# Down and output projection of a two-superblock trunk in the 4+4-sum seven-product form, with sums kept in PSUM, weight sums by DRAM transfers and activation sums made beside the up-projection

## The chip, the cores and the metric

The kernel runs on one core of a Trainium2 chip. The metric is the device time of one execution in microseconds; three runs of the kernel before gave a median of 2719.7 us (2719.38 to 2721.61). Engines are named as in the profile: PE does matmuls (PEld loads their weights), DVE, ACT and POOL work elementwise, SP only issues transfers. ACT and POOL issue transfers too, and all of these queues run in order.

## What is computed

One layer of a mixer block and a gated feed-forward network on a 2048 x 1024 input, in float32:

```python
xn = rmsnorm(x, norm1_g)
z = xn @ w_in                              # pool channels, q, f, i, o, gates
ya = pool_mixer(u_pool, ...) @ w_pa
yb = hgrn2_mixer(zq, zf, zi, zo, ...) @ w_pb
merged = gates[0] * ya + gates[1] * yb
x = x + merged @ w_o                       # output projection, 1024 x 1024
h = rmsnorm(x, norm2_g) @ w_up             # 1024 x 5632, then a causal conv of width 3
x = x + (silu(gate) * val) @ w_down        # down projection, 2816 x 1024
out = rmsnorm(x, final_g)
```

## The kernel before

**Stages.** The sequence is worked in two superblocks of 1024 rows, each of two blocks (`hf` 0 and 1) of 512 rows. For each superblock the stages are: `io` (two of the input projections, `proj_io`), `in` (14 units of the other input projections, with the recurrence and the pooling as tasks beside them), `pa` and `pb` (branch projections and gating), `wo` (output projection), `up` (22 units of the up-projection, with conv and gate in `emit_up`) and `dn` (down projection, with the final norm). All large products are done as seven half-size products (Strassen's or Winograd's form) of two-part float32r operands: an operand is cast to a high part on ACT and the low part is subtracted on DVE (`split`, L561 and L562, for activations; `Stream.convert`, L207 and L208, for weights), and each product of tiles takes three matmuls (`n_step`, `chain_t`).

**Weights.** `Stream` holds the planned order of all weight tiles. `load` (L185) issues a 128 x 512 tile (256 KB) into one of 8 `raw` buffers on the SP queue, `convert` makes `ops` from it, at most 4 tiles ahead of PE's use and in 6 buffers. For `wo` and `dn`, `plan_n_step` makes the sums of two weight quarters on POOL (L430), five per row step k. For `up` and the second superblock's `io` and `in`, the sums of weight quarters come from DRAM: the class `Sums` makes them with eight dependent transfers for each group of four units, four plain copies on ACT's queue (L263) and four adding transfers on POOL's queue (L260), each of about 1 MB. `Sums.make` starts a task for a whole weight matrix; the task runs one transfer every `SUM_LAG` = 4 ticks (a tick is six large matmuls), going over all groups before the next dependent step. The `up` sums (6 groups, tiles su0 to su5) start when the first `io` stage ends, the `io` and `in` sums (so, si) when the first `up` stage starts. A weight tile that needs sums that are not made finishes the whole task at once (`join`).

**Output and down projection.** `Rows` runs `wo` (4 row steps k) and `dn` (11 steps). `DOWN` and `W_OUT` list passes of one or two of the seven products M1 to M7. `make` adds or subtracts two activation tiles on POOL (L1010), five per k, and splits the result; `run` multiplies, and after the last k adds each product from PSUM into one to two of the four output quarters on DVE (L1038): 12 additions for each of 4 row tiles. The last `hold` steps of a pass are run row tile by row tile. The gated activations of `up` go to DRAM (`dg`, 44 tiles in each superblock) and are fetched again (`g`, L760).

**Order.** Tasks are stepped by ticks while PE's matmuls are recorded; a scheduler then orders the instructions of each engine by its own estimate of times. At run time each engine and each queue takes its instructions strictly in that order.

Of the kernel before, what the change touches and what calls it, by code (L numbers as in the profile page):

```python
# [33 lines left out]
B12, B22, B21, B11 = 0, 1, 2, 3  # L34
PROD = {
    "M1": ("M1", ((0, 0, 1), (1, 1, 1)), ((B11, 1), (B22, 1)), ((0, 0, 1), (1, 1, 1))),
    "M2": ("M2", ((1, 0, 1), (1, 1, 1)), ((B11, 1),), ((1, 0, 1), (1, 1, -1))),
    "M3": ("M3", ((0, 0, 1),), ((B12, 1), (B22, -1)), ((0, 1, 1), (1, 1, 1))),
    "M4": ("M4", ((1, 1, 1),), ((B21, 1), (B11, -1)), ((0, 0, 1), (1, 0, 1))),
    "M5": ("M5", ((0, 0, 1), (0, 1, 1)), ((B22, 1),), ((0, 0, -1), (0, 1, 1))),  # L40
    "M6": ("M6", ((1, 0, 1), (0, 0, -1)), ((B11, 1), (B12, 1)), ((1, 1, 1),)),
    "M7": ("M7", ((0, 1, 1), (1, 1, -1)), ((B21, 1), (B22, 1)), ((0, 0, 1),)),
}


def passes(*names):
    return [[PROD[n] for n in p.split()] for p in names]


DOWN = passes("M3 M6", "M5 M7", "M4 M1", "M2")  # L50
W_OUT = passes("M3 M5", "M7 M4", "M1", "M2", "M6")

# [14 lines left out]
LEADS = 2, 5, 4  # L67
# [7 lines left out]
SUM_LAG = 4  # L75
# [6 lines left out]
def tile_trunk(  # L82
# [37 lines left out]
    count = [0]  # L120
# [26 lines left out]
    def mm(*args, **kw):  # L147
        pe.matmul(*args, **kw)  # L148
        count[0] += 1
        if count[0] % MM_PER_TICK == 0:  # L150
            tick()
# [79 lines left out]

    stream = Stream()

    class Sums:


        def __init__(self, name, groups):

            self.name, self.groups = name, groups
            self.where = {}  # L240
            self.task = None
# [5 lines left out]
        def make(self):  # L247
            def gen():
                n = len(self.groups)
                for g, (units, _) in enumerate(self.groups):  # L250
                    for k in ("s1", "s2", "s3", "s4"):
                        nm = f"{self.name}{g}{k}"
                        self.t[g, k] = dram.tile([P, len(units), 512], F32, tag=nm, name=nm)
                for dst, src, add in (("s1", 2, 0), ("s3", 2, 0), ("s1", 3, 1), ("s3", 0, 1),
                                      ("s2", "s1", 0), ("s2", 0, 1), ("s4", "s2", 0),
                                      ("s4", 1, 1)):
                    for g in range(n):
                        x = self.t[g, src] if isinstance(src, str) else self.groups[g][1][src]
                        if add:
                            pool.dma_start(self.t[g, dst], x, accum_op=ALU.add)  # L260
                        else:
                            with tc.issue_after(stream.mark.ins):
                                act.dma_start(self.t[g, dst], x)  # L263
                        yield SUM_LAG

            self.task = Task(gen())
# [60 lines left out]
    def plan_mixer(b0):  # L327
# [8 lines left out]
        plan_n("wo", w_o, W_OUT, KD // 2)  # L336
# [63 lines left out]
    def plan_ffn():  # L400
# [6 lines left out]
        plan_n("dn", w_dn, DOWN, MF // 2)  # L407

    def plan_n(key, src, passes, nk):
        for prods in passes:  # L410
            for k in range(nk):
                plan_n_step(key, src[k], prods)

    def plan_n_step(key, rows, prods):
        where = {}
        for q in sorted({q for pr in prods for q, _ in pr[2]}):
            where[q] = stream.raw(rows[:, q * 512 : (q + 1) * 512])

        def view(q):
            return where[q].tile  # L420

        for pr in prods:
            terms = pr[2]

            def fn(nm, terms=terms):
                if len(terms) == 1:
                    return view(terms[0][0])
                t = slot(f"{nm}b")
                op = ALU.add if terms[1][1] > 0 else ALU.subtract
                pool.tensor_tensor(t, view(terms[0][0]), view(terms[1][0]), op)  # L430
                return t

            stream.op(key, fn, [where[q] for q, _ in terms])
# [11 lines left out]

    io_q = w_io.rearrange("k p c -> p k c")
    sums["up"] = Sums("su", [group_up(m0) for m0 in range(0, MF, GROUP)])
    sums["io"] = Sums("so", [(list(range(4)),
# [537 lines left out]
    class Rows:  # L986
        def __init__(self, name, key, passes, nk, get, acc, ahead=0):
            self.name, self.key, self.passes, self.nk = name, key, passes, nk
            self.get, self.acc, self.ahead = get, acc, ahead
            self.steps = [(i, k) for i in range(len(passes)) for k in range(nk)]  # L990
            self.made = 0
            self.a = {}

        def make(self, upto):
            while self.made < min(upto, len(self.steps)):
                i, k = self.steps[self.made]
                for n in range(self.made, min(self.made + self.ahead, len(self.steps))):
# [496 lines left out]
```

## Time and profile before

The profiled execution took 2723.2 us, of which the span (first to last instruction) is 2721.5 us. The table is read from the profile's view of busy time by stretches, cut at the first matmul of each stage.

| stage | superblock 0, us | superblock 1, us |
|---|---|---|
| start and `io` | 117 | 82 |
| `in` | 389 | 353 |
| `pa` and `pb` | 90 | 90 |
| `wo` | 92 | 92 |
| `up` | 468 | 446 |
| `dn` | 251 | 243 |
| after the last matmul | | 8.5 |

A stage is read by comparing it with the time of its own matmuls, and with the busy time of DVE and POOL in the same stretch. The share of the 16 transfer engines' time ("DMA share") and the granted PE clock stand in the same rows.

### The profile page before, as it was taken

The page shows a single profiled execution, that of the slowest core. Times are in us where ns is not written, and L with a number is a line of the kernel's source. Part 1 is how long each engine was busy: PE and PEld are TensorE (multiplying, and loading weights), DVE is VectorE, ACT ScalarE, POOL GpSimd, SP SyncE. Part 2 cuts the span into 40 slices and gives each one's busy share as a digit, 9 for nine tenths or more (in the row PEclk, how much of TensorE's full clock was granted, in tenths as well). Part 3 has the DMA queues.
Part 4 walks back from the last instruction along what each step waited for, and adds up shares of the span by engine and source line. Part 5 has one row for each costly group of instructions (what it writes and reads, how often), then busy time and mean ns, then how long its engine had stood idle before and what let it go on. Part 6 is the DMA issues. An engine that isn't in the chain of part 4 may idle for free.

```text
span 2721.5 us, 35290 instructions
## 1 busy us (share of the span) xinstructions
PE 2571.2 (94%) x11464; PEld 2072.5 (76%) x11464; DVE 2190.7 (80%) x3414; ACT 1166.9 (43%) x2204; POOL 1113.3 (41%) x1171
## 2 busy tenths in 40 slices
PE   7989998999799999989999999999999999998898
PEld 6777777887578888767878788888777888885686
DVE  7879779579687777799987777674898777778998
ACT  5324333423454444443364344342345544444344
POOL 5544344076442111197761111211853211117785
PEclk9999999999899999999999999999999999999999
DMA  6797569654999543474465344347443433436552
GB/s 213 216 265 194 153 192 236 212 192 153 284 262 284 165 127 118 143 262 132 159 198 159 97 124 128 113 150 246 164 146 94 126 121 123 121 123 227 196 168 85
DMA packets 254472, 467.50 MB, mean 172 GB/s; under 512 B 24688, under 2 KB 41200, under 8 KB 253936
## 3 DMA queue, kind: packets, MB, share of 16 engines
q1 hardware_dynamic: 207840, 356.08, 41.1%
q0 software_dynamic: 21184, 41.95, 8.7%
q10 hardware_dynamic: 25264, 67.23, 6.6%
q8 instruction: 90, 1.47, 0.2%
q14 instruction: 94, 0.77, 0.1%
HBM read 391.75 MB, written 157.29 MB: 202 GB/s over the span
## 4 chain that ended last, share of the span: by engine, by line
PE 60%; DVE 16%; DMA 7%; issue 5%; POOL 5%; ACT 2%; SPq 0%; ACTq 0%; DVEq 0%; POOLq 0%
PE up_Z L148 13%; PE up_X L148 8%; PE up_V L148 8%; DVE ops L208 5%; PE gr_Z L148 4%; PE pa L148 3%; PE pb L148 3%; PE gr_X L148 2%; PE gr_V L148 2%; PE dn_M L148 2%; PE fr_Z L148 2%; DMA g<-dg 1%; PE fr_X L148 1%; PE io_Z L148 1%; DMA su3s<-in_w_up_t 1%
## 5 line engine op out<-in xcount | busy, mean ns | idle before, releaser
L207 ACT CAST ops<-raw 128x512 fp32r<-128x512 f32 x582 | 358.5, 620 | 716.2 <-PE up_Z L148 240.0
L208 DVE TENSOR_TENSOR ops<-raw,ops 128x512 fp32r<-128x512 f32 x582 | 450.7, 780 | 124.1 <-ACT ops L207 119.1
L1296 POOL COPY hist<-h 128x2 f32<-128x2 f32 x88 | 38.3, 435 | 403.5 <-DVE h L942 402.9
L1301 DVE SCALAR_TENSOR_TENSOR e<-h,cols,e 128x512 f32<-128x512 f32 x176 | 136.3, 794 | 18.8 <-ACT e L1299 13.8
L1299 ACT ACTIVATE e<-h,cols 128x512 f32<-128x512 f32 x176 | 138.1, 812 | 19.0 <-DVE h L940 11.7
L1303 DVE SCALAR_TENSOR_TENSOR e<-h,cols,e 128x512 f32<-128x512 f32 x176 | 136.0, 777 | 1.3
L1294 POOL COPY h<-h 128x2 f32<-128x2 f32 x88 | 38.0, 458 | 152.1 <-DVE h L940 148.6
L1232 POOL TENSOR_TENSOR ya<-ya,gl 128x512 f32<-128x512 f32 x32 | 47.2, 1486 | 106.8 <-DVE gl L1231 106.8
L979 DVE TENSOR_TENSOR up_u<-up_Z,up_e 128x512 f32<-128x512 f32 x44 | 30.4, 690 | 66.8 <-PE up_Z L148 64.9
L1134 POOL TENSOR_TENSOR q<-q,qs 128x512 f32<-128x512 f32 x16 | 23.3, 1456 | 131.9 <-ACT qs L1133 94.1
L1307 ACT ACTIVATE e<-e 128x512 f32<-128x512 f32 x88 | 55.3, 629 | 40.6 <-DVE e L1303 40.6
L809 POOL COPY qm<-q 128x64 f32<-128x64 f32 x64 | 25.8, 457 | 109.5 <-DVE q L874 21.6
L1171 ACT ACTIVATE gt<-gt,cols 128x512 f32<-128x512 f32 x48 | 34.8, 726 | 74.0 <-DVE gt L942 58.0
L1038 DVE TENSOR_TENSOR ac<-ac,dn_M 128x512 f32<-128x512 f32 x96 | 59.9, 679 | 3.6 <-PE dn_M L148 3.6
L1038 DVE TENSOR_TENSOR x<-x,wo_M 128x512 f32<-128x512 f32 x96 | 61.1, 678 | 0.4
L940 DVE TENSOR_TENSOR h<-up_Z,up_e 128x512 f32<-128x512 f32 x44 | 30.4, 691 | 38.1 <-PE up_Z L148 38.0
L942 DVE TENSOR_TENSOR h<-up_u,up_V 128x512 f32<-128x512 f32 x88 | 60.0, 682 | 0.1
L817 PE MATMUL pl<-qm,k 128*128 128x192 f32 x256 | 48.7, 332 | 8.0 <-DVE f L835 3.1
L817 PEld LDWEIGHTS pl<-qm,k 128*128 128x128 f32 x256 | 43.1, 191 | 13.1 <-issue 4.6
L148 PE MATMUL dn_M<-ops,dn_M_0h 128*128 128x512 f32 x112 | 39.3, 425 | 13.9 <-DVE ops L208 5.5
L1294 POOL COPY h<-hist 128x2 f32<-128x2 f32 x88 | 52.2, 642 | 0.0
L1308 DVE TENSOR_TENSOR e<-e,e 128x512 f32<-128x512 f32 x72 | 51.6, 717 | 0.4
(1743 smaller groups left out, 9025.4 us busy)
## 6 DMA issues: line engine op xcount, KB each, us to landing
raw<-in_w_dn SPq DMA_DIRECT2D x198, 256.0 KB, 3.6
raw<-in_w_up_t SPq DMA_DIRECT2D x132, 256.0 KB, 3.2
raw<-in_w_in_t SPq DMA_DIRECT2D x98, 256.0 KB, 3.6
dg<-e SPq DMA_DIRECT2D x88, 256.0 KB, 3.5
g<-dg SPq DMA_DIRECT2D x88, 256.0 KB, 5.3
raw<-in_w_o SPq DMA_DIRECT2D x80, 256.0 KB, 3.6
raw<-in_w_io SPq DMA_DIRECT2D x68, 256.0 KB, 4.9
x<-in_x SPq DMA_DIRECT2D x64, 256.0 KB, 5.3
```

The lines of the kernel that those rows point to most:

```text
L148: pe.matmul(*args, **kw)
L207: self.mark = act.copy(hi, v)
L208: dve.tensor_tensor(lo, v, f32(hi), ALU.subtract)
L817: pe.matmul(pa_[:, c * 192 : c * 192 + 192], ks[:, (i + c) * P : (i + c + 1) * P], mv[:, c].rearrange("p s x -> p (s x)"), start=True, sto ...
L942: dve.tensor_tensor(dst, t, ps, ALU.add if how == "add" else ALU.subtract)
L1038: dve.tensor_tensor(t, t, ps[pr[0], j], ALU.add if sg > 0 else ALU.subtract)
L1294: pool.tensor_copy(h[:, 0:2], hist[:, mt] if hf == 0 else hs[s, 0][:, TB : TB + 2])
L1299: act.activation(t, h[:, 2:], AF.Identity, bias=col(o_cb + mt), scale=col(o_cw + 4 * MF + mt))
L1301: dve.scalar_tensor_tensor(t, h[:, 1 : 1 + TB], col(o_cw + 2 * MF + mt), t, ALU.mult, ALU.add)
L1303: dve.scalar_tensor_tensor(t, h[:, 0:TB], col(o_cw + mt), t, ALU.mult, ALU.add)
L1307: act.activation(g, g, AF.Silu)
L1308: (pool if m < G_POOL else dve).tensor_tensor(g, g, ts[0, hf], ALU.mult)
```

## The change

`wo` and `dn` use Winograd's form (products P1 to P7, four weight sums and four activation sums), in which partial sums of products stay in PSUM: a product either starts a bank set (A or B, four banks each) or goes on adding to it, and after each product its bank set is added to one to four output quarters. Per row tile there are 9 additions in `dn` and 11 in `wo` in place of 12.

- The weight sums of `wo` and `dn` become DRAM sums like the others (tiles sw and sd0 to sd2). All sums are now made by one task, `prepare`, in the order wo, up, dn, io, in; two groups are active at a time, one transfer every 9 ticks (54 large matmuls). A tile that needs a group that is not done steps this task until it is.
- The activation sums are made by `add_forms` on POOL: for `wo` in `evac_b` during `pb`, for `dn` in `glu` during `up`. All seven forms of `dn` go to DRAM (77 tiles in each superblock): P1, P2 and P4 by SP, the four sums by POOL's queue. The values of block 1 carry a minus sign, so its products are `scalar_tensor_tensor` on DVE.
- In `Rows`, only the passes that are named so hold back row tiles.

```diff
-        for prods in passes:
-            for k in range(nk):
-                plan_n_step(key, src[k], prods)
...
-                op = ALU.add if terms[1][1] > 0 else ALU.subtract
-                pool.tensor_tensor(t, view(terms[0][0]), view(terms[1][0]), op)
...
+                if p in R_ONE:
+                    c = R_ONE[p] * 512
+                    plan_one(key, src[k][:, c : c + 512])
+                else:
+                    plan_one(key, sums[key].of(k, R_SUM[p]))
...
+    def prepare():
+        todo = [sums[name].make(g) for name in ("wo", "up", "dn", "io", "in")
+                for g in range(len(sums[name].groups))]
+        active = []
+        while todo or active:
+            while todo and len(active) < 2:
+                active.append(todo.pop(0))
+            g = active.pop(0)
+            try:
+                lag = next(g)
+            except StopIteration:
+                continue
+            active.append(g)
+            yield lag
...
         def of(self, unit, key):
             def src():
-                join(self.task)
                 g, i = self.where[unit]
+                while g not in self.done:
+                    prep[0].step()
                 return self.t[g, key][:, i, :]
...
-SUM_LAG = 4
+SUM_LAG = 9
...
+            def step(j, k, w):
+                n_step(ps[j], w, self.a[p, k], j, new and k == 0, k == nk - 1,
+                       skip_group_check=True)
+                if k == nk - 1:
+                    for hf, c, sg in self.adds[p]:
+                        t = self.acc[hf, j, c]
+                        dve.tensor_tensor(t, t, ps[j], ALU.add if sg > 0 else ALU.subtract)
+                    done(j)
...
+    def add_forms(two, forms, k, name, store=lambda p, t: None):
+
+        def comb(p, x0, x1, op):
+            if (p, k) in forms or x0 is None or x1 is None:
+                return
+            t = slot(f"{name}_{p}_{k}")
+            pool.tensor_tensor(t, x0, x1, op)
+            forms[p, k] = t
+            store(p, t)
...
+        comb("P7", two.get((1, 0)), two.get((0, 0)), ALU.subtract)
+        comb("P5", two.get((0, 0)), two.get((0, 1)), ALU.subtract)
+        comb("P6", forms.get(("P5", k)), two.get((1, 0)), ALU.subtract)
+        comb("P3", forms.get(("P6", k)), two.get((1, 1)), ALU.add)
...
-                (pool if m < G_POOL else dve).tensor_tensor(g, g, ts[0, hf], ALU.mult)
...
+                if hf:
+                    dve.scalar_tensor_tensor(g, g, -1.0, ts[0, hf], ALU.mult, ALU.mult)
+                else:
+                    (pool if m < G_POOL else dve).tensor_tensor(g, g, ts[0, hf], ALU.mult)
...
+                    if p in R_FORM:
+                        stores.append((d, t))
+                    else:
+                        pool.dma_start(d, t)
...
-        down.run(0, 2, each0)
-        down.run(1, 2, each1)
-        down.run(2, 2, each2, lambda j: Task(final(0, j)))
+        down.run("P1", 0, each0)
+        down.run("P6")
+        down.run("P2", 0, each1)
+        down.run("P7")
+        down.run("P5", 0, each2)
+        down.run("P4", 2, done=lambda j: Task(final(0, j)))
         go_io[0] = False
-        down.run(3, 6 if last else 3, each3, lambda j: Task(final(1, j)))
+        down.run("P3", 6 if last else 3, each3, lambda j: Task(final(1, j)))
```

Three places show how instructions move. The first is POOL early in the second superblock's `dn`. Before, it holds weight sums (w, L430) and activation sums (dn2_M6, L1010):

```order
L430 TENSOR_TENSOR w735b_22695<-raw771_22558,raw772_22560 128x512
L430 TENSOR_TENSOR w736b_22712<-raw773_22623,raw771_22558 128x512
L1010 TENSOR_TENSOR dn2_M6_4s_22737<-g2_4_1_22448,g2_4_0_22446 128x512
L430 TENSOR_TENSOR w737b_22749<-raw774_22625,raw775_22627 128x512
L430 TENSOR_TENSOR w738b_22766<-raw776_22663,raw774_22625 128x512
L1010 TENSOR_TENSOR dn2_M6_5s_22791<-g2_5_1_22462,g2_5_0_22460 128x512
```

In the changed kernel POOL goes from the last unit of `up` (unit 21) straight to the small sums of the final norm:

```order
L1331 COPY h2_21_0_1_22484<-h2_21_0_0_22419 128x2
L1333 COPY hist_121<-h2_21_0_1_22484 128x2
L1360 DMA dg2_P6_10_22459<-gf2_P6_10_22457 128x512
L1056 TENSOR_TENSOR gf2_P3_10_22501<-gf2_P6_10_22457,e2_21_1_1_22494 128x512
L1360 DMA dg2_P3_10_22503<-gf2_P3_10_22501 128x512
L1404 TENSOR_TENSOR fss2_0_0_24094<-fss2_0_0_24094 128x1
```

So POOL has no 128 x 512 sum left in `dn` until the final norm. The second place is POOL in a unit of the second superblock's `up` (unit 15). Before, it has only the two-column copies of the conv's history:

```order
L1294 COPY h2_15_0_0_21451<-hist_121 128x2
L1294 COPY h2_15_1_0_21475<-hist_121 128x2
L1296 COPY hist_121<-h2_15_1_1_21432 128x2
L1294 COPY h2_15_1_1_21432<-h2_15_1_0_21475 128x2
L1294 COPY h2_15_0_1_21502<-h2_15_0_0_21451 128x2
L1296 COPY hist_121<-h2_15_0_1_21502 128x2
```

In the changed kernel, the sums (gf) and their stores stand between these copies:

```order
L1333 COPY hist_121<-h2_15_1_1_21340 128x2
L1331 COPY h2_15_1_1_21340<-h2_15_1_0_21475 128x2
L1056 TENSOR_TENSOR gf2_P5_7_21393<-e2_14_1_0_21218,e2_15_1_0_21386 128x512
L1360 DMA dg2_P5_7_21395<-gf2_P5_7_21393 128x512
L1056 TENSOR_TENSOR gf2_P6_7_21397<-gf2_P5_7_21393,e2_14_1_1_21251 128x512
L1331 COPY h2_15_0_1_21418<-h2_15_0_0_21359 128x2
L1333 COPY hist_121<-h2_15_0_1_21418 128x2
L1360 DMA dg2_P6_7_21399<-gf2_P6_7_21397 128x512
L1056 TENSOR_TENSOR gf2_P3_7_21435<-gf2_P6_7_21397,e2_15_1_1_21428 128x512
L1360 DMA dg2_P3_7_21437<-gf2_P3_7_21435 128x512
```

For every two units, four sums and four transfers are added to POOL. The third place is ACT in the first superblock's `dn`, around the second pass. Before, there are only casts of weights (ops) and activations:

```order
L207 CAST ops337_10691<-w337b_10689 128x512
L207 CAST ops338_10708<-w338b_10706 128x512
L561 CAST dn0_M6_6h_10733<-dn0_M6_6s_10731 128x512
L207 CAST ops339_10745<-w339b_10743 128x512
L207 CAST ops340_10762<-w340b_10760 128x512
```

In the changed kernel (ops336 is the weight of P6's first step, ops337 to ops339 those of its next ones) two copies of the weight sums of `dn` stand between them:

```order
L204 CAST ops336_10693<-raw322_10448 128x512
L261 DMA si0s1_10698<-in_w_in_t 512x1x512
L572 CAST dn0_P6_1h_10719<-g0_P6_1_10559 128x512
L261 DMA sd1s4_9816<-sd1s2_9814 16x16384
L204 CAST ops337_10729<-raw323_10504 128x512
L204 CAST ops338_10752<-raw324_10527 128x512
L261 DMA sd2s4_9932<-sd2s2_9930 16x12288
L572 CAST dn0_P6_2h_10742<-g0_P6_2_10604 128x512
```

The copy of sd1s4 reads sd1s2, which an adding transfer on POOL's queue must have finished.

More of the change, by code (lines that the diff above doesn't have):

```diff
@@ L119, in tile_trunk @@
     tasks = []
-    count = [0]
+    count = [0, None]
     class Task:
@@ L986, in tile_trunk, with __init__ @@
     class Rows:
[L987 to L990, printed above, removed]
-            self.made = 0
-            self.a = {}
+        def __init__(self, name, key, how, nk, form, acc, ahead=0):
+            self.name, self.key, self.nk, self.form, self.acc = name, key, nk, form, acc
+            self.order, self.bank_of, self.new, self.adds = how
+            self.ahead = ahead
+            self.steps = [(p, k) for p in self.order for k in range(nk)]
+            self.made = 0
+            self.a, self.raw, self.ps = {}, {}, {}
@@ L994, in make, with get @@
+        def get(self, step):
+            if step not in self.raw:
+                self.raw[step] = self.form(*step)
+            return self.raw[step]
         def make(self, upto):
             while self.made < min(upto, len(self.steps)):
-                i, k = self.steps[self.made]
-                for n in range(self.made, min(self.made + self.ahead, len(self.steps))):
-                    i2, k2 = self.steps[n]
-                    for pr in self.passes[i2]:
-                        for hf, kh, _ in pr[1]:
-                            self.get(k2 + self.nk * kh, hf)
@@ L1102, in mixer @@
         if b0 == 0:
-            sums["up"].make()
+            prep.append(Task(prepare()))
         queue = []
```

231 lines of the change are left out of this document (114 added, 117 removed).

## The prediction

> **What bounds the kernel now.** I read the page's totals first, then busy time by stage, then who waits for whom in the stages that the change touches, then single instructions there.
>
> ```profile
> span 2721.5 us, 35290 instructions
> PE 2571.2 (94%) x11464; PEld 2072.5 (76%) x11464; DVE 2190.7 (80%) x3414; ACT 1166.9 (43%) x2204; POOL 1113.3 (41%) x1171
> ```
>
> PE is busy 94% of the span, so all that any other engine can give back is some 150 us. Where it lies shows the view by stretches, cut at the stages. Columns after the length: busy time and count of PE, PEld, DVE, ACT and POOL, granted clock, DMA share, GB/s. The rows are `in`, `wo`, `up`, `dn` of superblock 0, then of superblock 1, and last a long undisturbed piece of the second `up`.
>
> ```profile
> 117.00:506.00 389.00, 359.20 (x1764) 295.76 (x1763) 307.51 (x682) 140.72 (x318) 149.18 (x163) 0.98 0.78 209
> 596.00:688.00 92.00, 85.83 (x371) 66.75 (x369) 90.41 (x106) 37.64 (x72) 64.58 (x52) 0.98 0.46 149
> 688.00:1156.00 468.00, 441.93 (x1881) 354.89 (x1882) 346.67 (x509) 221.96 (x367) 112.90 (x181) 0.97 0.70 196
> 1156.00:1407.00 251.00, 230.69 (x954) 179.24 (x953) 243.06 (x231) 113.86 (x220) 203.49 (x157) 0.97 0.58 191
> 1489.00:1842.00 353.00, 349.57 (x1769) 293.12 (x1768) 259.04 (x669) 143.48 (x318) 55.14 (x86) 0.99 0.42 127
> 1932.00:2024.00 92.00, 84.87 (x369) 66.26 (x367) 90.97 (x106) 37.39 (x72) 64.63 (x52) 0.98 0.45 141
> 2024.00:2470.00 446.00, 436.48 (x1882) 352.03 (x1883) 343.38 (x508) 221.40 (x367) 99.84 (x161) 0.99 0.40 122
> 2470.00:2713.00 243.00, 224.89 (x924) 175.76 (x922) 237.90 (x217) 102.12 (x188) 196.72 (x138) 0.97 0.50 168
> 2075.00:2430.00 355.00, 351.82 (x1515) 285.24 (x1514) 270.53 (x407) 174.06 (x277) 66.44 (x119) 1.00 0.40 122
> ```
>
> The last row gives PE's pace: 355 us for 1515 large matmuls at clock 1.00, 0.2343 us each. `dn` has 7 x 11 x 4 x 3 = 924 of them, 216.5 us; it takes 251 and 243. `wo` has 336, 78.7 us; it takes 92. In these four stages **DVE is the limit**: 243 of 251, 238 of 243, and 90 and 91 of 92 us. The waits of PE and of its weight loads in the second `dn` say the same:
>
> ```profile
> PE dn_M L148 <- DVE ops L208: 10.0, 9, 3.2
> PEld dn_M L148 <- DVE ops L208: 14.1, 9, 3.6
> ```
>
> Why DVE is full shows the order in time of DVE and, below it, of POOL, in a piece of that stage (start, length, instruction):
>
> ```profile
> 2601.37 0.68 DVE L562 TENSOR_TENSOR dn_M_10l<-dn_M_10s,dn_M_10h 128x512 fp32r<-128x512 f32 x1
> 2604.89 0.68 DVE L208 TENSOR_TENSOR ops<-w770b,ops 128x512 fp32r<-128x512 f32 x1
> 2606.09 1.78 DVE L562 TENSOR_TENSOR dn_M_1l<-g,dn_M_1h 128x512 fp32r<-128x512 f32 x1
> 2607.80 1.78 DVE L562 TENSOR_TENSOR dn_M_1l<-dn_M_1s,dn_M_1h 128x512 fp32r<-128x512 f32 x1
> 2609.50 1.79 DVE L562 TENSOR_TENSOR dn_M_2l<-g,dn_M_2h 128x512 fp32r<-128x512 f32 x1
> ```
> ```profile
> 2605.70 1.62 POOL L430 TENSOR_TENSOR w771b<-raw,raw 128x512 f32<-128x512 f32 x1 [1.89 <-DVE ops L208]
> 2607.29 1.74 POOL L430 TENSOR_TENSOR w772b<-raw,raw 128x512 f32<-128x512 f32 x1
> 2608.99 1.75 POOL L430 TENSOR_TENSOR w773b<-raw,raw 128x512 f32<-128x512 f32 x1
> ```
>
> The same subtraction takes 0.68 us while POOL is idle and 1.78 while POOL sums: the two run in lockstep. An addition with one operand in PSUM is not touched; its mean over `dn` is that of the free case:
>
> ```profile
> L1038 DVE TENSOR_TENSOR ac<-ac,dn_M 128x512 f32<-128x512 f32 x96 | 59.9, 679 | 3.6 <-PE dn_M L148 3.6
> ```
>
> **The change, part by part.** The terms are differences of stages of the profiled execution: 2721.5 us of span, 2723.2 in all, which is 3.5 above the median of 2719.7.
>
> *`dn` without POOL's sums.* Ten POOL sums per row step go. Two groups of subtractions get short: in the second `dn`, L208 (first row) and L562 (second):
>
> ```profile
> 2470.00:2713.00 243.00, 102.29 (x76) 0.97 0.50 168
> 2470.00:2713.00 243.00, 96.09 (x75) 0.97 0.50 168
> ```
>
> At 0.68 each they cost 103 us in place of 198, and 36 additions replace 48 (12 x 0.679 = 8 us less). DVE falls from 238 to about 135 us, 60% of the stage. PE is late next. Its 216.5 us, plus the start of the stage and the bunch of 12 additions after P1, where no row tile is held back (8 us on DVE, most of it beside P6's first steps): I take 221, **22 us less**. The first `dn` would give the same (251 to 229); what its transfers take back is the next part.
>
> *Sums in DRAM, first `dn`.* By the order and the tick counts, the groups sd1 and sd2 are not done when P6's fifth weight tile is asked for, 42 matmuls into P1, and eleven steps are then issued at once. PE reaches that tile 138 matmuls later (32 us). The chain is a plain copy, then an adding transfer; such take, median from issue to landing:
>
> ```profile
> su1s<-in_w_up_t POOLq DMA_DIRECT2D x4, 1024.0 KB, 15.7
> su0s<-su0s ACTq DMA_DIRECT2D x2, 7.8
> ```
>
> 7.8 + 15.7 = 23.5 us, and 16 more if two adding transfers run at once. Then the load of the tile, cast and subtraction:
>
> ```profile
> raw<-in_w_dn SPq DMA_DIRECT2D x198, 256.0 KB, 3.6
> ```
>  Worse, ACT holds the copy sd1s4, which waits for the same adding transfer, ahead of the casts of P6's steps 1 to 3; PE wants the first of these 24 us after the burst. So the stall is between 0 and 20 us (23.5 + 16 + 5 less 24); I take 8, nearer to the undisturbed 23.5 + 5 - 24 = 5. Behind ACT's waiting copy stand casts, behind SP's waiting load stand the fetches of activations, so both are late together and the stall is counted once. Bandwidth is the second price. The queues' totals (SP, POOL, ACT) are
>
> ```profile
> q1 hardware_dynamic: 207840, 356.08, 41.1%
> q0 software_dynamic: 21184, 41.95, 8.7%
> q10 hardware_dynamic: 25264, 67.23, 6.6%
> ```
>
> 44 adding transfers took 8.7% of 2721.5 = 237 us of all engines, 5.4 each; ACT's queue 2.7 us per MB. About 14 adding transfers and 13 copies fall into this stage: 76 + 35 = 111 us, beside the 0.58 x 251 = 146 us that it moves now. That is 257 us of transfers in 229 us of matmuls. Not all have to land there (`io` needs only so), so between 0 and 28 us; with the stall I take 12 in all. First `dn`: 251 - 22 + 12 = 241, **10 less**.
>
> The Trainium skill speaks against the change here: DMA: Bandwidth & Descriptors, section "Issuing engines are not separate DMA queues", says that transfers started by ACT, SP or POOL end up on the same 16 engines and interleave. By it moving sums onto other queues frees nothing, and the whole 28 us would be paid (first `dn` 257); the 0.78 share of `in` above, where adding transfers ran, neither proves nor denies it. It is rival B.
>
> *`wo`.* Five sums of weights and five of activations per step leave this stage too; 56 subtractions at 0.68 and 44 additions at 0.68 are 68 us of DVE, with 3 us of other work 71 in place of 90. But P1's 16 additions (11 us) stand in one bunch on DVE ahead of the weight of P5's second step, and P5 needs P1's banks; with the splits before them I reckon 4 to 5 us of stall. The 32 transposes in the stage (L610, PE and PEld) are pipelined and stay; I count 3 to 4 us of them:
>
> ```profile
> 596.00:688.00 92.00, 5.22 (x32) 3.91 (x32) 0.98 0.46 149
> ```
>
> 78.7, 3.5 and the stall make 87: **5 to 5.5 less, twice: 11.** The forms are made on POOL in `pb`, beside the gating additions, which cost
>
> ```profile
> L1232 POOL TENSOR_TENSOR ya<-ya,gl 128x512 f32<-128x512 f32 x32 | 47.2, 1486 | 106.8 <-DVE gl L1231 106.8
> ```
>
> 16 of these and 16 sums at the same 1.49 are 48 us in `pb`'s 45. The last forms end some 8 us late, and P6 first wants them 11 us after `pb` (48 matmuls of P1). If that cover fails, it costs up to 5 us.
>
> *First `up`.* 468 against 446 us for the same matmuls. The difference has a name:
>
> ```profile
> PE up_Z L148 <- ACT m_T21h L561: 11.6, 1, 11.6
> PE up_V L148 <- DVE m_T10l L562: 4.5, 1, 4.5
> ACT m_T21h L561 <- DMA si2s<-in_w_in_t: 13.1, 1, 13.1
> ```
>
> ACT held a transfer of the `in` sums that could not be issued, with a cast behind it. Those sums are gone from there; the ones that take their place come at 9 ticks and two groups. Between 0 and 22; I take 22 less, without the price of the next part: **18 with it**.
>
> *Forms made beside `up`.* 44 POOL sums and 44 POOL transfers are added in each `up`. A sum costs DVE up to 1.79 - 0.68 = 1.1 us when it meets a two-operand subtraction or conv step: at most 48 us. Four products of block 1 move from POOL to DVE and the rest turn into the slower kind:
>
> ```profile
> L1303 DVE SCALAR_TENSOR_TENSOR e<-h,cols,e 128x512 f32<-128x512 f32 x176 | 136.0, 777 | 1.3
> ```
>
> at most 18 x 0.1 + 4 x 0.78 = 5 us. DVE goes from 343 to at most 396 of 446 us: still below PE. Between 0 and 15 for chains that get longer; **4 more, each**. On SP, 33 more stores and 33 more fetches, less 22 loads, per superblock lie beside this.
>
> *`in`.* In the first, adding transfers make POOL wait with its weight sums behind them:
>
> ```profile
> POOL su3s L260 <- DMA su3s<-in_w_up_t: 18.2, 2, 11.8
> POOL su0s L260 <- DMA su0s<-in_w_up_t: 12.9, 2, 8.2
> ```
>
> 22 transfers replace 48 there, with 25 us between dependent ones. It is 36 us longer than the second; POOL's own weight sums remain in it. Between 0 and 25; **12 less**. Into the second `in` go the sums si1 to si3, with a second burst at the end of `io` (138 matmuls ahead of use, ACT and POOL waiting as above): 0 to 20; **8 more** with `io`.
>
> Sum: -22 - 10 - 11 - 18 + 4 - 12 + 8 = **-61**: span 2660.5, median 2719.7 - 61 = **2659**.
>
> **Rivals.** B: transfers limit. Both bursts cost 20 and the first `dn` pays all 28 us: +16 on `dn`, +12 on `in`, and nothing gained in the first `in` is +12: 2699. For it: 257 us of transfers in 229. Against: loads are issued eight tiles ahead, 22 us.
> C: all bursts are hidden (-12 and -8), and the first `in` gains 20 (-8): 2631. For it: the waits of POOL quoted last.
> D, the slower side: DVE becomes the limit of `up`. If POOL's stores held DVE as its sums do, 88 instructions at 1.79 us would put DVE at 343 + 157 + 5 = 505 us, 59 over 446 in each: 2719.7 - 47 (the terms without `up`'s) - 22 (the wait that goes) + 118 = about 2769. It decides once an added POOL instruction costs DVE over (446 - 348) / 88 = 1.1 us. Against it: a sum costs at most that, and POOL's 20 adding transfers in the first `up` leave L208 as it is in the second, which has none:
>
> ```profile
> 688.00:1156.00 468.00, 107.70 (x151) 0.97 0.70 196
> 2024.00:2470.00 446.00, 108.40 (x151) 0.99 0.40 122
> ```
>
> The Trainium skill bears on D: SBUF — State Buffer, "Who interferes with whom", lets a DVE instruction with two SBUF inputs collide only with a POOL instruction that reads SBUF. The rows above agree for sums (1.78 against 0.68); by it the stores would cost DVE nothing and D would not be reached. No row here shows a store of tiles by POOL.
> E: the change does not free DVE, since something else fills it: about 2718. The lockstep rows speak against it.
>
> **How the numbers follow.** Forecast 0.57 (2640 to 2685), B 0.20, C 0.12, D 0.06, E 0.05. The range reaches from C's 2631 to B's 2699, a little beyond each: 2626 to 2702. It leaves out D and E and the ends. A measurement of this kernel tells 0.2% (5.4 us) from no change: faster 0.89, same 0.05, slower 0.06.
>
> **What would show it.** L208 and L562 near 0.69 us mean in both `dn`, DVE about 60% busy there, the second `dn` at 219 to 224 us. `wo` at 87, with PE waiting for DVE around P5. In the first `dn` one wait of 5 to 15 us on a cast behind a copy of sd1s or sd2s, or on its weights. The first `up` without the 11.6 us wait; DVE at 370 to 396 us in both. I am wrong if L208 stays near 1.1 us in `dn`, if DMA share there is 0.95 or more with PE waiting for raw tiles, or if `up` grows past 460.

## The result

The changed kernel takes **2832.25 us** (median of four runs, 2829.11 to 2835.99), the kernel before 2720.65 in the same session: ratio 1.041, 95% interval 1.0392 to 1.0428. It is 112 us slower; 61 us less had been forecast. The profiled run took 2835.99 us, with a span of 2834.3.

The page of the changed kernel (busy time, share of the span and instructions of each engine):

```profile
span 2834.3 us, 35362 instructions
PE 2597.9 (92%) x11464; PEld 2087.6 (74%) x11464; DVE 1945.2 (69%) x3390; ACT 1168.8 (41%) x2204; POOL 798.8 (28%) x1087
```

DVE lost 245 us of work and POOL 315 against before, and still the span grew. The view by stretches of the changed kernel shows where (busy time and count of PE, PEld, DVE, ACT, POOL, granted clock, DMA share, GB/s): `wo`, `up`, `dn` of the first superblock, then of the second.

```profile
586.00:681.00 95.00, 84.90 (x366) 67.60 (x365) 78.44 (x117) 41.04 (x84) 33.74 (x39) 0.95 0.69 209
682.00:1195.00 513.00, 455.48 (x1876) 357.23 (x1875) 346.14 (x507) 220.90 (x356) 156.72 (x248) 0.95 0.66 180
1196.00:1465.00 269.00, 231.25 (x958) 182.97 (x956) 148.36 (x222) 112.66 (x217) 47.79 (x67) 0.94 0.96 295
2008.00:2092.00 84.00, 82.33 (x369) 66.15 (x370) 73.67 (x114) 42.20 (x86) 19.80 (x30) 1.00 0.39 126
2092.00:2602.00 510.00, 453.63 (x1880) 355.75 (x1879) 346.46 (x510) 222.70 (x361) 136.42 (x231) 0.96 0.40 122
2602.00:2826.00 224.00, 217.27 (x927) 175.03 (x925) 137.49 (x204) 100.80 (x187) 21.67 (x34) 0.98 0.60 201
```

The second `dn` does what was forecast: DVE at 61% and the stage down to 224 us. The two `up` stages take 513 and 510 us in place of 468 and 446, with DVE at 346, where it was. No engine there is full: PE is idle for 56 us of the second `up` in place of 10, and its own products take 17 us longer (the last section says why), together the 64 us. PE's waits in the second `up` (total, times, longest), first of the changed kernel, then of the kernel before:

```profile
PE up_X L145 <- ACT up_e L984: 24.4, 10, 6.4
PE up_Z L145 <- DVE up_u L986: 14.7, 1, 14.7
PE up_Z L145 <- DVE up_u L990: 14.3, 19, 0.8
```
```profile
PE up_X L148 <- ACT up_e L973: 3.2, 1, 3.2
PE up_Z L148 <- DVE up_u L975: 3.2, 1, 3.2
```

up_e is the first copy of a unit (e1, out of P1's bank, which P2 goes on adding to), up_u are u2 and u3. One such place in order of time, PE and ACT of the changed kernel (start, length, instruction):

```profile
2298.84 0.39 PE L145 MATMUL up_V<-m_T13h,ops 128*128 128x512 f32 x1
2301.26 0.50 PE L145 MATMUL up_X<-m_f4h,ops 128*128 128x512 f32 x1 [2.03 <-ACT up_e L984]
...
2303.49 0.63 PE L145 MATMUL up_X<-m_f6h,ops 128*128 128x512 f32 x1
```
```profile
2297.25 0.60 ACT L204 CAST ops<-raw 128x512 fp32r<-128x512 f32 x1
2299.31 0.62 ACT L204 CAST ops<-raw 128x512 fp32r<-128x512 f32 x1 [1.46 <-issue]
2300.11 0.63 ACT L1344 ACTIVATE e<-e 128x512 f32<-128x512 f32 x1 [0.18 <-DVE e L1340]
2300.64 0.57 ACT L984 COPY up_e<-up_X 128x512 f32<-128x512 f32 x1
```

P1's last product had started at 2293.3 and ended at 2293.7. The copy could have run seven us earlier; it stands behind the silu (L1344) of the unit before, which waits for that unit's conv on DVE. In the kernel before, at the same unit, the copy runs 3.5 us ahead of the silu:

```profile
2204.23 0.56 ACT L973 COPY up_e<-up_X 128x512 f32<-128x512 f32 x1
...
2207.78 0.63 ACT L1307 ACTIVATE e<-e 128x512 f32<-128x512 f32 x1
```

The built order (the order in which the program lists each engine's instructions) says the same for every unit from the fifth on. ACT around e1 of unit 10 in the kernel before has silu behind the copy, in the changed kernel ahead of it (the changed kernel's rows):

```
L1336 ACTIVATE e2_9_1_1_20390<-h2_9_1_1_20302,cols_84 128x512
L204 CAST ops653_20538<-raw639_20337 128x512
L204 CAST ops654_20577<-raw640_20372 128x512
L1344 ACTIVATE e2_9_1_1_20390<-e2_9_1_1_20390 128x512
L984 COPY up2_10_e1_20421<-up2_10_X_20401 128x512
```

On DVE, u2 moved behind the last product of the unit before (L1346) in the same way. The diff touches neither the copy nor u2. What it does touch is the number of tiles: those of the units all come from one pool, `N_SLOTS = 77`, of which the forms of the input hold 7 x 4 x 2 = 56 through `up`. The other 21 turn over. Two units took 22 tiles (e1, u2, u3, four h, four e each) and now take 26, with the four sums. That is **theory S** (shortage): a tile for e1 is not to be had until the unit before has given one back, so the placing of instructions puts e1 behind the work that frees it. Rivals: **P**, the work of the sums and stores on POOL; **T**, the transfers of weight sums.

### The profile page after: what moved, and what is told of

Read it like the earlier page. It is cut to its first block, busy times and chain, and to the rows that moved or that the text cites. A ratio compares the mean times of both kernels' runs of the same rounds, so it can differ in the third digit from the quotient of the medians.

```text
span 2834.3 us, 35362 instructions
## 1 busy us (share of the span) xinstructions
PE 2597.9 (92%) x11464; PEld 2087.6 (74%) x11464; DVE 1945.2 (69%) x3390; ACT 1168.8 (41%) x2204; POOL 798.8 (28%) x1087
## 5 line engine op out<-in xcount | busy, mean ns | idle before, releaser
L204 ACT CAST ops<-raw 128x512 fp32r<-128x512 f32 x732 | 450.7, 619 | 1064.1 <-PE up_Z L145 203.6
L205 DVE TENSOR_TENSOR ops<-raw,ops 128x512 fp32r<-128x512 f32 x732 | 540.9, 744 | 378.1 <-ACT ops L204 372.9
L1056 POOL TENSOR_TENSOR gf_P<-e,e 128x512 f32<-128x512 f32 x44 | 58.0, 1319 | 186.1 <-DVE e L1346 123.6
L145 PE MATMUL up_X<-m_f4h,ops 128*128 128x512 f32 x88 | 41.0, 466 | 48.6 <-ACT up_e L984 48.6
L1056 POOL TENSOR_TENSOR gf_P<-gf_P,e 128x512 f32<-128x512 f32 x44 | 57.6, 1309 | 85.3 <-DVE e L1346 85.0
L1344 ACT ACTIVATE e<-e 128x512 f32<-128x512 f32 x88 | 55.1, 627 | 29.8 <-DVE e L1340 28.8
L145 PE MATMUL up_Z<-m_T40h,ops 128*128 128x512 f32 x88 | 38.5, 437 | 28.4 <-DVE up_u L990 28.4
L145 PE MATMUL up_Z<-m_T30h,ops 128*128 128x512 f32 x88 | 36.3, 417 | 29.4 <-DVE up_u L986 29.4
L1032 DVE TENSOR_TENSOR x<-x,wo_P 128x512 f32<-128x512 f32 x88 | 56.5, 689 | 9.2 <-PE wo_P L145 8.9
L145 PEld LDWEIGHTS up_X<-m_f4h,ops 128*128 128x128 f32 x88 | 17.9, 203 | 60.4 <-ACT up_e L984 57.2
L1032 DVE TENSOR_TENSOR ac<-ac,dn_P 128x512 f32<-128x512 f32 x72 | 46.5, 685 | 17.3 <-PE dn_P L145 17.1
```

The costliest lines, as they stand in the source:

```text
L145: count[1] = pe.matmul(*args, **kw)
L204: self.mark = act.copy(hi, v)
L205: dve.tensor_tensor(lo, v, f32(hi), ALU.subtract)
L1032: dve.tensor_tensor(t, t, ps[j], ALU.add if sg > 0 else ALU.subtract)
L1056: pool.tensor_tensor(t, x0, x1, op)
L1344: act.activation(g, g, AF.Silu)
```

## Experiments in `up`

Four runs. First, buffers of their own for the sums (two raw buffers make the room):

```diff
-N_RAW = 8
+N_RAW = 6
+    gfp = ctx.enter_context(tc.tile_pool(name="gfp", bufs=2))
...
-            t = slot(f"{name}_{p}_{k}")
+            if name[:2] == "gf":
+                t = gfp.tile([P, TB], F32, tag="gf", name=f"{name}_{p}_{k}")
+            else:
+                t = slot(f"{name}_{p}_{k}")
```

> The changed kernel, with the four sums that each pair of up-projection units makes put into two buffers of their own instead of the shared pool of 77 (two raw buffers are given up for the room, 6 stay). Theory S (shortage of buffers): in the changed kernel the sums take 26 buffers per pair of units instead of 22 out of the 21 that the 56 forms leave free, so the copy e1 of the next unit gets no buffer until the last product of this one is placed; it then stands behind that unit's silu on ACT, and u2 behind the product on DVE, and PE waits. With their own buffers both stand ahead again: the two up stages fall from 514 and 510 us to 450-475 each, and the kernel to 2715-2770 us. Theory P (the work itself: 44 added POOL instructions a superblock beside DVE, and 88 stores issued by POOL): nothing of that work is taken away, the up stages stay within 10 us of 514 and 510, the kernel at 2820-2845. Theory T (the transfers of weight sums, the rival in which transfers limit): the same as P.

Measured: 2708.18 us, ratio to before 0.9957 (0.994 to 0.9973), a little below the range expected. The `up` stages take 459 and 448 us. ACT of this run, at the same unit:

```profile
2218.08 0.57 ACT L986 COPY up_e<-up_X 128x512 f32<-128x512 f32 x1
2218.55 0.62 ACT L206 CAST ops<-raw 128x512 fp32r<-128x512 f32 x1
2221.09 0.62 ACT L206 CAST ops<-raw 128x512 fp32r<-128x512 f32 x1 [1.92 <-PE up_Z L147]
2223.64 0.63 ACT L1349 ACTIVATE e<-e 128x512 f32<-128x512 f32 x1 [1.93 <-DVE e L1345]
```

The copy runs 5.6 us ahead of the silu, and of the waits of PE for up_e in the second `up` one is left:

```profile
PE up_X L147 <- ACT up_e L986: 3.1, 1, 3.1
```

Second, no buffer more, but the sums asked for later:

```diff
-                add_forms(two, gt, k, f"gf{b0}", store)
+                sums_due.append((two, gt, k, f"gf{b0}", store))
...
             u.after(p)
+            if p in ("P6", "P7", "P4"):
+                late_sums()
```

> The changed kernel, with the sums of a pair of units emitted after the next unit's P6, P7 or P4 instead of right behind the product that they need, in the shared pool as before and with 8 raw buffers. Theory S: e1 and u2 ask for their buffers first and are placed ahead of silu and product again; up stages 445-475 us each, the kernel 2710-2760. Theory P: the same instructions run a third of a unit later, up stages stay above 500, the kernel at 2820-2845. Theory T: as P.

Measured: 2731.74 us, `up` 464 and 462. Third, the sums left out; plain products are stored in their place, so the stores stay:

```diff
-                add_forms(two, gt, k, f"gf{b0}", store)
+                for p, at in (("P1", (1, 0)), ("P2", (1, 1)), ("P4", (0, 1)), ("P7", (0, 0)),
+                              ("P5", (0, 0)), ("P6", (0, 1)), ("P3", (1, 1))):
+                    if (p, k) not in gt and at in two:
+                        gt[p, k] = two[at]
+                        store(p, two[at])
```

> The changed kernel with the four sums of each pair left out: plain products are stored in the place of the sums, so the number of stores and what POOL issues is the same (the output of the down-projection differs from the reference). Theory S: up stages 440-470 us each, at most 12 us a stage below the run with buffers of their own; the kernel 2700-2760. Theory P: also down to 2700-2760, but about 50 us a stage below the run with buffers of their own, since here the work is gone and there it isn't. Theory T: the kernel stays within 20 us of 2832.

Measured: 2698.71 us, `up` 451 and 447, which is 8 and 1 us below the run with buffers of their own (6 raw buffers there, 8 here). So the work of the sums costs about that much, and P falls. Fourth, the reverse, in the kernel before: four more tiles, called for where the changed kernel makes its sums (the same two lines for P7, P5, P6 and P3), with an addition of one column in each:

```diff
+                t = slot(f"{name}_{p}_{k}")
+                pool.tensor_tensor(t[:, 0:1], x0[:, 0:1], x1[:, 0:1], ALU.subtract)
```

> The kernel before, unchanged but for four buffers more per pair of up-projection units: each is taken at the place where the changed kernel makes its sums, and written by POOL in one column of 512 (an addition of 128x1), which reads the same tiles; nothing uses them. Theory S: the shortage alone moves e1 behind silu and u2 behind the product, and the up stages of 468 and 446 us grow by 30-65 each; the kernel 2780-2850. Theory P: 88 additions of one column cost nothing that can be seen, the kernel stays within 6 us of 2720. Theory T: as P.

Measured: 2816.57 us, ratio 1.0362 (1.0346 to 1.0377), `up` 515 and 494 in place of 468 and 446. All of the loss is in these two stages, and the waits are the changed kernel's:

```profile
PE up_X L148 <- ACT up_e L973: 18.2, 10, 6.3
PE up_Z L148 <- DVE up_u L979: 14.1, 18, 0.8
PE up_Z L148 <- ACT e L1325: 12.5, 1, 12.5
```

Four tiles per two units, with next to no work in them, make the old kernel 99 us slower. The built orders say the same: e1 stands behind the silu of the unit before from the fifth unit on in the changed kernel and in this run, and in no unit of the kernel before, of the run with own buffers and of the run with the later sums. With the two runs that give the tiles back in different ways, theory S is shown; T falls as the cause of `up` too: none of the four runs touches the transfers of weight sums.

## Experiments in the other stages

The table has start-to-start times of the stages as differences from before, in us, beside the prediction's terms. "Own" is the run with own buffers, "lag 7" and "none" are below.

| stage | forecast | changed | own | lag 7 | none |
|---|---|---|---|---|---|
| first `in` | -12 | -28 | -26 | -22 | -29 |
| first `pa` + `pb` | 0 | +14 | +11 | +17 | +1 |
| first `wo` | -5.5 | +4 | +4 | 0 | -8 |
| first `up` | -18 | +47 | -9 | -17 | -19 |
| first `dn` | -10 | +18 | +22 | -14 | -29 |
| second `io` + `in` | +8 | +17 | +13 | -2 | -2 |
| second `wo` | -5.5 | -8 | -7 | -7 | -8 |
| second `up` | +4 | +65 | +2 | +2 | +4 |
| second `dn` | -22 | -20 | -29 | -29 | -30 |

What is left beside `up` lies in the first superblock and at the start of the second, where the weight sums are transferred. The first `dn` of the changed kernel by stretches, and ACT in it:

```profile
1196.00:1230.00 34.00, 27.23 (x107) 21.09 (x106) 23.10 (x30) 14.17 (x24) 11.59 (x13) 0.90 1.01 290
1230.00:1265.00 35.00, 22.23 (x80) 16.64 (x78) 12.88 (x22) 6.53 (x12) 4.63 (x4) 0.85 1.05 329
1265.00:1300.00 35.00, 31.04 (x119) 24.43 (x120) 16.25 (x26) 10.69 (x20) 2.30 (x2) 0.90 1.10 280
```
```profile
1243.38 0.58 ACTq L261 DMA_DIRECT2D si0s<-in_w_in_t  x1
1243.99 0.62 ACT L572 CAST dn_P_1h<-g_P 128x512 fp32r<-128x512 f32 x1 [15.26 <-DMA ac<-dx]
...
1252.91 0.51 ACTq L261 DMA_DIRECT2D sd2s<-sd2s  x1
1253.45 0.62 ACT L572 CAST dn_P_2h<-g_P 128x512 fp32r<-128x512 f32 x1 [6.33 <-DMA raw<-sd1s]
```

The transfers fill all 16 engines (share 1.01 to 1.10), and ACT stands still for 15.3 us (until a load of ac has landed) and 6.3 us ahead of two issues, with the casts behind them. PE's waits for these casts are shorter (the second row adds an earlier wait of 2.0 us to one of 2.5 here):

```profile
PE dn_P L145 <- ACT ops L204: 7.6, 1, 7.6
PE dn_P L145 <- ACT dn_P_2h L572: 4.5, 2, 2.5
```

Neither stop ended with the landing of data that a copy reads: by the trace's landing times, the adding transfers that sd1s4 and sd2s4 wait for had landed by 1235.2 and 1241.0. In the built program the load of ac, the copy of si0 and that of sd2s4 count their landings on the same one of eight semaphores, and each is issued only when the one before it has landed: the copy of si0 (1243.38) after the load of ac, that of sd2s4 (1252.91) when the copy of si0 had landed, 9.5 us after its issue. No run changes this sharing.

The next four runs all have the sums' own buffers. Their theory D says that the transfers of weight sums lengthen the stages into which they fall (it is not the prediction's rival D); theory E, that the stages are held by other loads.

```diff
-SUM_LAG = 9
+SUM_LAG = 7
```

> The kernel with buffers of its own for the sums (2708 us), with one weight-sum transfer every 7 ticks of 6 matrix products instead of 9: the 24 steps of the down-projection's weights then end before its first stage begins, where they were forced out together in it. Theory D (transfers of weight sums that fall into the first down-projection make its excess: 273 us against 214 for the second): first dn 273 -> 245-260, second in 366 -> 355-363, first in +0 to +8, first pa and pb +0 to +4; the kernel 2680-2698. Theory E (that stage is held by its own loads, activations and next rows, and not by the sums): first dn stays 266 or more, the kernel 2700-2715.

Measured: **2650.22 us, ratio 0.9749 (0.9727 to 0.977)**: first `dn` 237, second `in` 351, first `in` 367.5. All but the last are better than expected, the total by 30 us. Same stage, first three stretches:

```profile
1131.00:1166.00 35.00, 30.32 (x116) 23.66 (x115) 24.31 (x34) 16.93 (x29) 10.33 (x11) 0.90 0.95 267
1166.00:1201.00 35.00, 35.00 (x153) 28.24 (x152) 21.05 (x34) 12.77 (x22) 2.32 (x2) 1.00 1.06 342
1201.00:1236.00 35.00, 35.00 (x153) 28.42 (x152) 17.98 (x29) 15.03 (x27) 2.18 (x2) 1.00 1.03 319
```

The DMA share is as high as it was, and yet PE is full: what costs is not how much is transferred but which transfers somebody waits for.

No transfers of weight sums while the first superblock's `pa` to `wo` and `dn` run:

```diff
-SUM_LAG = 9
+SUM_LAG = 5
...
         for t in list(tasks):
+            if paused[0] and t in prep:
+                continue
```

> The same with one transfer every 5 ticks, and none in the first superblock's pa, pb, wo and dn stages. Theory D: pa and pb 51 and 50 -> 45-47 each, wo 96 -> 86-90, first dn 273 -> 225-240, second in 355-366; the denser transfers cost first in 0-15 and first up 0-10; the kernel 2650-2690. Theory E: dn 260 or more, pa and pb unchanged, the kernel 2700-2725.

Measured: 2661.91 us: `pb` 46, `wo` 86, `dn` 223 as theory D has it, but `pa` 50, first `in` 378, first `up` 470. Next, no such transfers at all; where a sum would be read, a quarter of the weights is read instead:

```diff
                 g, i = self.where[unit]
-                while g not in self.done:
-                    prep[0].step()
-                return self.t[g, key][:, i, :]
+                return self.groups[g][1][0][:, i, :]
...
-            prep.append(Task(prepare()))
```

> The kernel with buffers of its own for the sums, without any of the 112 weight-sum transfers: where a sum would be read, a quarter of the weights themselves is read, the same bytes (the output differs from the reference). Theory D: the floor of every stage of the first superblock: pa and pb 45-46, wo 85-88, first dn 222-232, first in 340-358, first up 447-455, second in 340-356; the kernel 2610-2650. Theory E: first dn 260 or more, pa, pb and wo within 3 us of 51, 50 and 96.

Measured: 2611.5 us; by stages, the last column of the table. The transfers (60 copies and 60 adding ones in the program, not the 112 of the expectation) cost 97 us in the run with own buffers (2708 less 2611), 51 of them in the first `dn`; at 7 ticks 39 are left.

The last of the four puts POOL's work back beside DVE in `dn`:

```diff
             v = fn(f"w{j}")
+            if key == "dn":
+                x = gfp.tile([P, TB], F32, tag="gf", name=f"extra{j}")
+                pool.tensor_tensor(x, v, v, ALU.add)
```

> The kernel with buffers of its own for the sums, with an addition of 128x512 on POOL, which nothing uses, added for each of the 77 weight tiles of the down-projection and the second down-projection's as well. The prediction's term (POOL's work slows DVE's subtractions from 0.7 to 1.8 us and so makes the second dn longer: 22 us for the 110 additions of before): the mean of the weight subtraction there rises from 0.73 to 1.2-1.7 us and the second dn from 214 to 222-236 us; the kernel 2718-2745. Rival (DVE has time to spare there, the gain came from fewer products of the matrix engine or from loads): the mean may rise, the stage stays within 5 us of 214, the kernel within 12 of 2708.

Measured: 2735.56 us, the second `dn` 228.5 in place of 213.9, the first 288 in place of 273. The subtraction there in the run without the additions (first line) and with them:

```profile
L207 DVE TENSOR_TENSOR ops<-raw,ops 128x512 fp32r<-128x512 f32 x72 | 52.8, 734 | 47.5 <-ACT ops L206 43.8 <-DMA raw<-sd0s 2.1
```
```profile
L202 POOL TENSOR_TENSOR extra<-raw 128x512 f32<-128x512 f32 x74 | 98.3, 1338 | 77.2 <-DMA raw<-sd0s 20.8 <-DMA raw<-in_w_dn 19.5 <-DMA raw<-sd2s 17.2
L210 DVE TENSOR_TENSOR ops<-raw,ops 128x512 fp32r<-128x512 f32 x73 | 61.1, 843 | 44.5 <-ACT ops L209 44.1
```

Its mean goes from 0.73 to 0.84 us, less than the 1.2 to 1.7 expected; the stage grows by 14.6 all the same. The direction is the prediction's, but DVE is not full here (158 of 228.5 us): PE waited twice, 8.6 us together, for a subtraction and a cast, and its products took 219.9 us at a mean clock of 0.97 in place of 213.9 at 1.00, which makes the other 6. The additions also hold the raw tiles longer, which this run does not separate.

Four more runs looked for a better spacing: 6 ticks with a pause in `pa` and `pb`, the same with `wo`, and 8 and 6 ticks without any pause.

> Sums in buffers of their own, one weight-sum transfer every 6 ticks, and none in the first superblock's pa and pb. By theory D and the stages measured so far: pa and pb 55.8 and 50.6 (a transfer every 7 ticks) -> 46-48 each, wo 90-95, first in 370-375, first up 452-462, first dn 237 or less, second in 351; the kernel 2636-2652 us against 2650 without the pause. If pa and pb are long for another reason than the transfers in them, they stay near 55 and 50 and the kernel at 2648-2660.

> The same with none in the first wo either: 12 steps fewer are done when the first dn begins, its own end 20 us ahead of it. wo 91.5 -> 85-87 us, first up 455-465, first dn 235-242; the kernel 2634-2650 us. If the steps kept out of wo cost as much in up and dn as they gave, 2645-2660.

> Buffers of their own for the sums, a weight-sum transfer every 8 ticks. The last of the down-projection's sums is then issued as its first stage begins (one step is forced there, not eleven), and some of the second input projection's are still forced at its start. Theory D: first dn 273 (at 9) -> 240-252, second in 360-366 as at 9; the kernel 2668-2685. If the steps' number per time matters and not when they come, halfway between 9 and 7: 2678 +-6, with first dn about 255 and second in about 358.

> The same, every 6 ticks: nothing is forced anywhere, fewer steps are left for the first dn, more fall into the first in, pa, pb, wo and up. Theory D: first dn 230-237, second in 351, first in 368-373, pa 55-58, up 452-462; the kernel 2645-2662, so no more to be had from this number. A steady gain with fewer ticks would give 2620-2635.

Measured: 2662.22, 2658.38, 2681.31 and 2658.85 us. With the pause `pa` and `pb` are 46 to 47 each and `wo` 84 to 85, as without any transfer, so the transfers are what lengthens them. But the first `up` grows to 468 and 472 (451 at 7 ticks) and the first `dn` to 245 and 248: the first total lies above both ranges that were expected, the second in the range for the case that the steps cost as much later as they gave. The cost moves on. The longest stall of `up` in the first of them, 11 us, starts on POOL and passes over DVE (second fence) and ACT to PE:

```profile
1110.05 1.25 POOL L1064 TENSOR_TENSOR gf_P<-gf_P,e 128x512 f32<-128x512 f32 x1 [12.09 <-DMA dg_P<-gf_P]
...
1112.16 0.31 POOL L1341 COPY h<-hist 128x2 f32<-128x2 f32 x2
```
```profile
1112.39 0.75 DVE L1348 SCALAR_TENSOR_TENSOR e<-h,cols,e 128x512 f32<-128x512 f32 x1 [8.97 <-POOL h L1341]
```

A sum had to wait 12.1 us until the store of an earlier one had left one of the two buffers, and the conv's history copies stand behind it on POOL. So two buffers are scarce as soon as transfers crowd `up`; whether a third would repair the pause was not tried.

At 8 ticks the first `dn` is 244 and the second `in` still 371 (some of its sums are forced there), at 6 ticks 221 and 350, with `pa` and `pb` 56 each and `up` 462; both totals are in their ranges. Of 6, 7, 8 and 9 ticks without a pause, 7 is the best.

## Why the prediction was wrong

- **Forms made beside `up`, "4 more, each": the step that failed.** It weighed the added work against DVE's and POOL's time, and the work does fit: DVE is busy for 346 us in the changed kernel and 366 in the run with own buffers, at most 396 in the forecast, and without the sums the stages are only 8 and 1 us shorter. "Between 0 and 15 for chains that get longer" left out that the sums need room: four more tiles out of a full pool changed the order on ACT and DVE, and PE waits for the unit before. In place of +4 each this made the stages 55 and 62 us longer than with buffers of their own (+47 and +65 against before). With those buffers the second `up` is as forecast, +2.
- **First `up`, -18.** The wait of 11.6 us that was to go did go. With own buffers -9 is left of the -18, at 7 ticks -17.
- **Rival D** had the right side and stage, but not the mechanism: DVE is not full, and POOL's stores cost it nothing. The run without the sums keeps all stores, and the second `up` has 0.71 us per weight subtraction and 0.75 per conv step there (0.72 and 0.76 before). This agrees with the Trainium skill (SBUF — State Buffer, "Who interferes with whom"), by which a DVE instruction with two SBUF inputs collides with a POOL instruction that reads SBUF. The sums do cost DVE time where they meet it: 0.90 us per conv step in the run with own buffers.
- **First `dn`, -10: a mis-sized term.** The transfers cost 51 us there in the run with own buffers, where 12 were taken. In the changed kernel the stall behind ACT's copies was near the size taken, PE's 7.6 and 2.5 us against 8; with own buffers PE waits 14.8 us for the first of these casts alone. But its cause was another, the shared semaphore and not the adding transfer, and the longer stop stood at the issue of a copy (si0) for which no wait had been seen. The rest of the 51 was not traced wait by wait. By the Trainium skill (DMA: Bandwidth & Descriptors, "Issuing engines are not separate DMA queues") transfers from all three engines interleave on the same 16 engines; the shares of 1.01 to 1.10 agree. A first `dn` of 257 us, rival B's price for this, was still too low (269). Once the transfers came earlier, 237.
- **Rival B** has the size of what is left: without the shortage, at 9 ticks, the kernel takes 2708, and B's sum was 2699 (it counts the 28 us of bandwidth in the first `dn`, but not the 20 us of a stall beside them, which its condition names).
- **`pa` and `pb`: a term left out**, +14. They load activations back from DRAM, and in the changed kernel casts wait longer for those loads while the sums run (before, at most 4.4 us):

```profile
ACT oTs_1h L572 <- DMA oT<-od: 8.1, 1, 8.1
...
ACT mxs_2h L572 <- DMA mx<-md: 4.7, 1, 4.7
```

  Without transfers nearly all of the excess is gone. PE's own waits for such casts are only 2.7 and 2.3 us; the rest of the 14 was not traced to single waits.
- **`wo`**: -8 in the second (-5.5 forecast; PE waits 2.9 us there, less than the 4 to 5 reckoned), +4 in the first, where transfers run.
- **Second `io` and `in`, +8**: +17, and -2 once nothing is forced there. **First `in`, -12**: -28, beyond the 25 that bounded it, and no more without any transfer (-29).
- **Second `dn`, -22: right in the mechanism, -20.** The subtractions of weights (first row) and activations (second) take 0.72 and 0.70 us in place of 1.35 and 1.28, and DVE is 61% busy, as foretold:

```profile
2602.00:2826.00 224.00, 51.92 (x72) 0.98 0.60 201
2602.00:2826.00 224.00, 52.30 (x75) 0.98 0.60 201
```

  That the number fits as well is in part luck. With the order in `up` restored it is -29: PE is then busy without a break for 213.9 us, less than the 216.5 that the forecast took as its floor, while in the changed kernel it waits 6.4 us for two casts, the longer time (5.2) for one that stands behind the last unit's silu. POOL's part in it is shown in direction; the run that put 77 additions back returned 14.6 us.

With own buffers and 7 ticks the total is near the forecast, 2650 against 2659, but partly by luck: single terms miss by up to 17 us, the +17 of `pa` and `pb` made up for by more gained elsewhere. That version beats both kernels.

## What to carry to other kernels

Count tiles as well as time: a change that adds four live tiles to a full pool can reorder engines that it does not touch, so compare the built order wherever the pool is shared, not only where instructions are added. If a stage slows with no engine full, look at what stands ahead of the late instruction on its own engine. In this kernel, background transfers cost least when they were done before a stage that is short of bandwidth, and the trace speaks against issuing them from an engine whose other work PE waits for, since the issue can wait for a landing that has nothing to do with it (another issuer was not tried).

## What the runs showed of the hardware

A short pause of PE can cost more than its length. After the pause of 2.0 us shown above, seven matmuls followed each other at 0.43 us in place of 0.23; the view by stretches has the granted clock at 0.66 there, and at 1.00 right behind:

```profile
2301.00:2306.00 5.00, 4.74 (x14) 3.74 (x15) 1.06 (x2) 0.30 (x2) 2.15 (x4) 0.66 0.47 160
2306.00:2320.00 14.00, 13.21 (x58) 10.42 (x57) 10.94 (x17) 7.16 (x11) 1.58 (x4) 1.00 0.27 76
```

That is some 1.6 us on top of the pause. It does not follow every pause: the second `up` of the changed kernel has eight pauses of 2.0 us, and six of them were followed by such a run of slow matmuls, two by none; nor were the 21 pauses of 0.8 to 1.7 us there. What decides between them is not shown. Slow matmuls make some 13 of the 17 us by which PE's busy time in the second `up` is longer, 454 us in the changed kernel and 436 before, for the same products.
